# A two-layer trunk on one core: the order of loads in the S5 blocks, and the place of the y sums and low parts behind the retention masks

## The chip, the core and the metric

The kernel runs on one core of one Trainium2 chip. The metric is the device time of one launch in microseconds (us). TensorE is PE in the rows, VectorE is DVE, ScalarE is ACT, GpSimd is POOL and SyncE, whose queue issues nearly all DMAs, is SP.

## What is computed

The input is one sequence of 1024 frames with 1024 features, in fp32. Two layers are added to it, `x = x + mixer(rmsnorm(x))`, and a last rmsnorm follows. The change touches the mixer of the first layer only. Cut to what matters, it is:

```python
proj = h @ w_in                       # u, g_s5, q, k, v, g_ret
y_s5 = s5_mixer(u_s5, ...)            # diagonal complex state space, 64 groups of 16 channels
                                      # y = gelu(C x + D u); y = y * sigmoid(y @ glu_w + glu_b)
y_s5 = y_s5 * silu(g_s5)
y_ret = retention(q, k, v) * silu(g_ret)
#   scores = (q k^T) * mask;  out = scores v + (decayed q) S;  S = decay * S + kv
#   out = (out - mean) * rsqrt(var + eps), per head
return concat([y_s5, y_ret]) @ w_out
```

The second layer is a Conformer convolution module with its own projections. It stands behind all that the change touches.

## The kernel before

All of it is one class, `Trunk`. Each fp32 product is made as three products of high and low parts (`mm3`, L200 to L202: high by high, low by high, high by low), in matmuls of 128x512. An array so has a high tile (`...h`) and a low tile (`...l`), the low one being the array minus the high one.

The order of the work on each engine is not written out: a scheduler of the tile framework places the instructions by priorities and by the time of a simulated run. The code steers it with `tc.issue_after(x)`: what is issued inside that context stands behind `x`. The loads go through one queue, SP's, in the order that the scheduler gives, and each load also waits until its buffer is free (`bufs` in the tile calls).

**S5 blocks.** The state space part works in eight blocks of eight groups, while TensorE also makes the gate products `mm_g` of the input projection. For block B, `s5_states` (from L842) does this:

- it loads u (`U`, L850) from DRAM;
- TensorE makes the inputs of the states, `v`, from U and the tables W2 (L868), VectorE turns them (`m`, L876 to L881), scans them (L883) and turns them back into S (L890 to L895);
- TensorE makes a block of the convolution kernel, `kp` (L902, L903), VectorE adds the direct path to it (`Kg`, L906), TensorE transposes it (`kt`, L908), ScalarE copies it (`Kt`, L910), SP stores it to DRAM (`k_d`, L912), and a load with overlapping rows brings it back as the shifted kernel `Wd` (L915), which ScalarE copies to W1 (L917).

`s5_out` makes the block's y from W1, U, W3 and S one block later and stores it. The tables W2 of blocks 2 to 7 come from `s5_w2` (L791): four loads of 256 KB spread two small tables over the partitions (`PTr`, `PTi` at L799, `BTr`, `BTi` at L802), and six VectorE products (L806 to L811) make `W2r` and `W2i`. Each of these tiles has one buffer. The loads stand behind `self.u_load`, the load of U of the block before.

**Retention pairs.** The eight heads are worked in four pairs. `retention` (L997) makes k, q and v of a pair and then calls `ret_heads`: the scores `sp` (L1192) in two halves of the sequence, their masks on VectorE (`sc`, L1198), the output `ro` from states (L1221) and from scores (L1226), and statistics, normalization and transposes (`st`, `mv`, `on`, `rt`). `self.masked[0]` and `self.masked[1]` are the last mask of the first and of the second half. `kraw`, `krot`, `qraw` and `qrot` are the parts of the rotary embedding, `kt` at L1158 is the decayed k, and S (L1183, L1185) the state.

**The y pass.** Between the pairs the S5 output is read again, in four passes of two row blocks (`y_pass`, L947), each in three parts that are separated by `yield`: load and gelu, with the result stored to `yn_d` (L960); four sums for a Strassen-like product (L966 to L969), made in place, so that the first of them must wait until the store of `yn` has read its tile; and the split of the sums into a high part `th` (L973) and a low part (L974), both stored to `t_d` (L975, L976). In pair 2 the sums are made from `scored()` (L1029), which `ret_heads` calls when the masks of the first half have been written.

**The GLU.** `layer0_back_and_layer1` (L1264) multiplies y by the GLU weights. It loads the first quarter `y11` and the second quarter `y21` of y from `yn_d` (`load_split`, L1274: f at L1284, high part on ScalarE and low part on VectorE at L1260 and L1262), and sums of y from `t_d` (`load_sum`, L1296: `yt2`, `yt3`, 16 loads in all). The low parts of `y21` stand behind `self.last_kt`, the last `kt` of the last pair. The products with y21 are the first `mm_glu` behind the last `ro`.

## Time and profile before

| | us |
|---|---|
| runs | 1145.49, 1145.79, 1152.16; median 1145.79 |
| span of the profiled execution | 1149.0, 3.2 above the median |
| PE busy | 1125.3 (98% of the span) |
| DVE busy | 847.4 (74%) |
| POOL busy | 654.3 (57%) |
| ACT busy | 489.5 (43%) |
| longest wait of PE by line | 6.8 in two waits, at `ro` for the masks |
| mean rate of the DMA engines | 228 GB/s |

In a row of the timeline stand the start, the duration, the engine, the line and operation, what is written and read, how many instructions the row holds, and in brackets how long the engine had been idle and what ended that. A row of the waits has the engine and line that waited, what it waited for, and then the total, the number of times and the longest wait. A row of the windows has the stretch and its length, busy time with the number of instructions for PE, its weight loads, DVE, ACT and POOL, then the clock that TensorE was granted (1.00 is full speed), the mean busy share of the 16 DMA engines, and the GB/s that they moved.

### The profile page before, as it was taken

What the parts mean: (1) busy time and instruction counts of PE and PEld (TensorE: products, weight loads), DVE (VectorE), ACT (ScalarE), POOL (GpSimd) and SP (SyncE); (2) the same over time, 40 slices, a digit from 0 to 9 for tenths busy, and PEclk for the clock granted to TensorE, in tenths of its full rate; (3) what the DMA queues carried; (4) which work ended last, traced back from release to release, by engine and by line L of the source; (5) the groups of instructions that cost most, each with busy time, mean ns of one, the idle gap of its engine ahead of it and who ended that gap; (6) DMA issues with size and microseconds to landing.
All of it is one profiled execution on the core that took longest, in us unless ns stands there. A gap on an engine that the chain in (4) does not pass through costs nothing.

```text
span 1149.0 us, 17198 instructions
## 1 busy us (share of the span) xinstructions
PE 1125.3 (98%) x6286; PEld 986.1 (86%) x6286; DVE 847.4 (74%) x1464; ACT 489.5 (43%) x719; POOL 654.3 (57%) x448
## 2 busy tenths in 40 slices
PE   9999999999999999989899999999999999999997
PEld 7888878888888889889788888888888888888787
DVE  6975788887418469484669622599999889999844
ACT  6423222333223231322446523555545677444674
POOL 2059999999246354232476011489544568677663
PEclk9999999999999999989899999999999999999999
DMA  9344445556388766858999988665778755357865
GB/s 352 111 134 154 122 164 177 179 174 206 114 279 290 241 220 186 292 171 304 348 382 308 342 287 282 185 240 202 239 256 293 242 188 175 119 182 257 287 226 193
DMA packets 117636, 261.45 MB, mean 228 GB/s; under 512 B 10672, under 2 KB 42288, under 8 KB 116912
## 3 DMA queue, kind: packets, MB, share of 16 engines
q1 hardware_dynamic: 114096, 247.78, 64.1%
q10 hardware_dynamic: 3456, 12.58, 2.9%
q8 instruction: 49, 0.80, 0.3%
q14 instruction: 35, 0.29, 0.1%
HBM read 181.48 MB, written 74.65 MB: 223 GB/s over the span
## 4 chain that ended last, share of the span: by engine, by line
PE 74%; DVE 13%; DMA 5%; issue 3%; POOL 3%; ACT 2%; SPq 0%; POOLq 0%; DVEq 0%; ACTq 0%
DVE cv L1535 5%; PE mm_wo L201 5%; PE mm_wo L200 5%; PE mm_wo L202 5%; PE mm_g L200 4%; PE mm_g L201 4%; PE mm_g L202 4%; PE mm_b L201 2%; PE mm_b L202 2%; PE mm_b L200 2%; PE mm_a L202 2%; PE mm_a L201 2%; PE mm_a L200 2%; PE mm_u L202 2%; PE mm_u L200 2%
## 5 line engine op out<-in xcount | busy, mean ns | idle before, releaser
L1535 DVE SCALAR_TENSOR_TENSOR cv<-u,convw,cv 128x512 f32<-128x512 f32 x398 | 273.0, 748 | 6.8 <-ACT cv L1514 4.8
L1508 POOL TENSOR_TENSOR tp<-tp,tp 128x512 f32<-128x512 f32 x64 | 82.9, 1296 | 33.9 <-ACT tp L1507 32.8
L200 PE MATMUL mm_g<-xh,wh_g 128*128 128x512 f32 x256 | 99.4, 388 | 0.0
L201 PE MATMUL mm_g<-xl,wh_g 128*128 128x512 f32 x256 | 98.1, 383 | 0.0
L202 PE MATMUL mm_g<-xh,wl_g 128*128 128x512 f32 x256 | 97.9, 382 | 0.0
L437 POOL TENSOR_TENSOR s1q<-s1q,s1q 128x512 f32<-128x512 f32 x12 | 17.1, 1427 | 81.4 <-ACT s1q L432 81.4
L1507 ACT ACTIVATE tp<-u,convw 128x512 f32<-128x512 f32 x64 | 45.4, 719 | 35.6 <-POOL tp L1508 34.8
L200 PEld LDWEIGHTS mm_g<-xh,wh_g 128*128 128x128 f32 x256 | 48.8, 191 | 8.7 <-issue 1.2
L202 PEld LDWEIGHTS mm_g<-xh,wl_g 128*128 128x128 f32 x256 | 48.8, 191 | 7.1
L201 PEld LDWEIGHTS mm_g<-xl,wh_g 128*128 128x128 f32 x256 | 48.7, 190 | 6.9 <-issue 0.4
L190 POOL TENSOR_TENSOR wl_v<-wf_v,wh_v 128x1024 fp32r<-128x1024 f32 x12 | 31.0, 2590 | 38.0 <-ACT wh_v L189 38.0
L190 POOL TENSOR_TENSOR wl_glu<-wf_glu,wh_glu 128x1024 fp32r<-128x1024 f32 x14 | 35.1, 2506 | 30.7 <-ACT wh_glu L189 30.7
L202 PE MATMUL mm_oc<-zh,wl_woc 128*128 128x512 f32 (+1 forms) x144 | 51.0, 357 | 0.3 <-DMA wl_woc<-lo_woc 0.3
L201 PE MATMUL mm_oc<-zl,wh_woc 128*128 128x512 f32 (+1 forms) x144 | 51.1, 356 | 0.0
L200 PE MATMUL mm_oc<-zh,wh_woc 128*128 128x512 f32 (+1 forms) x144 | 50.7, 363 | 0.0
L201 PE MATMUL mm_u<-xl,wh_u 128*128 128x512 f32 x128 | 48.5, 381 | 0.7 <-DVE xl L316 0.7
L200 PE MATMUL mm_wo<-ysh,wh_wos 128*128 128x512 f32 x128 | 48.9, 382 | 0.0
L200 PE MATMUL mm_g<-h1h,wh_cg 128*128 128x512 f32 x128 | 48.9, 382 | 0.0
L201 PE MATMUL mm_b<-h1l,wh_cb 128*128 128x512 f32 x128 | 48.7, 381 | 0.1
L202 PE MATMUL mm_b<-h1h,wl_cb 128*128 128x512 f32 x128 | 48.6, 380 | 0.0
L201 PE MATMUL mm_wo<-ysl,wh_wos 128*128 128x512 f32 x128 | 48.5, 379 | 0.0
L202 PE MATMUL mm_wo<-ysh,wl_wos 128*128 128x512 f32 x128 | 48.5, 379 | 0.0
(526 smaller groups left out, 3613.3 us busy)
## 6 DMA issues: line engine op xcount, KB each, us to landing
wf_g<-w_ab SPq DMA_DIRECT2D x16, 512.0 KB
wf_wos<-w_out SPq DMA_DIRECT2D x16, 512.0 KB
wf_wor<-w_out SPq DMA_DIRECT2D x16, 512.0 KB
wf_cb<-w_c SPq DMA_DIRECT2D x16, 512.0 KB
wf_ca<-w_c SPq DMA_DIRECT2D x16, 512.0 KB
wf_woc<-w_out_c SPq DMA_DIRECT2D x16, 512.0 KB
wf_v<-w_v SPq DMA_DIRECT2D x12, 512.0 KB
wf_cg<-w_c SPq DMA_DIRECT2D x11, 512.0 KB
```

The source lines that it names most:

```text
L190: self.low_made = lo[i].tensor_tensor(wl[:].rearrange(fl)[:, c], wf[:, c], h.bitcast(F32), op=ALU.subtract)
L200: nc.tensor.matmul(ps, wh[:, kb, :], xh, start=start, stop=False, **more)
L201: nc.tensor.matmul(ps, wh[:, kb, :], xl, start=False, stop=False, **more)
L202: self.last_mm = nc.tensor.matmul(ps, wl[:, kb, :], xh, start=False, stop=stop, **more)
L437: nc.gpsimd.tensor_tensor(a, a, sq[:], op=ALU.add)
L1507: nc.scalar.mul(sk[:], u[:, k:k + HALF], cw[:, nb, k:k + 1])
L1508: gp.tensor_tensor(s0[:], s0[:], sk[:], op=ALU.add)
L1535: v.scalar_tensor_tensor(dst[:], *tap, accs_[i][:], op0=ALU.mult, op1=ALU.add)
```

## The change

Four edits, all of them to what stands behind what:

1. The load of the shifted kernel is kept as `self.wd_load`. The load of U stands behind the shifted kernel of the block before it, and the four loads of the W2 tables stand behind the last load of U and the last load of a shifted kernel.
2. In pair 2 the sums of y stand behind the masks of the second half, and are issued when these have been written.
3. The low parts of y21 stand behind the masks of the last pair's second half.
4. The loads of the sums `yt2` and `yt3` stand behind the last load of y21.

No instruction is added or removed apart from how DMA rows are grouped.

```diff
@@ plan
-        self.low_load, self.early_low = {}, None
+        self.low_load, self.early_low, self.wd_load = {}, None, None
@@ s5_w2
-        with self.tc.issue_after(self.u_load.ins):
+        with self.tc.issue_after(self.u_load.ins), self.tc.issue_after(self.wd_load.ins):
@@ s5_states
-        self.u_load = nc.sync.dma_start(U[:], self.u_d[B].rearrange("j h g m -> (j h) g m"))
+        with self.tc.issue_after(self.wd_load.ins) if self.wd_load else nullcontext():
+            self.u_load = nc.sync.dma_start(U[:], self.u_d[B].rearrange("j h g m -> (j h) g m"))
...
-        nc.sync.dma_start(Wd[:], bass.AP(tensor=kd.tensor, offset=kd.offset, ap=[[P, P], [16 * P, 8], [1, P]]))
+        self.wd_load = nc.sync.dma_start(
+            Wd[:], bass.AP(tensor=kd.tensor, offset=kd.offset, ap=[[P, P], [16 * P, 8], [1, P]]))
@@ retention, scored()
-                    with self.tc.issue_after(self.masked[0].ins):
+                    with self.tc.issue_after(self.masked[1].ins):
@@ ret_heads
-            if hf == 0:
+            if hf == 1:
                 scored()
@@ load_split
-                nc.sync.dma_start(f, part)
+                self.part_load = nc.sync.dma_start(f, part)
@@ load_sum
-        def load_sum(name, i, c, h):
+        def load_sum(name, i, c, h, behind=None):
...
-                    nc.sync.dma_start(o[:].bitcast(F32), self.t_d[i, j, rows(k), hs(c)])
+                    with self.tc.issue_after(behind.ins) if behind else nullcontext():
+                        nc.sync.dma_start(o[:].bitcast(F32), self.t_d[i, j, rows(k), hs(c)])
...
-        b11, b21 = load_split(B(0, 0), "y11", 0, True, None, self.last_v), load_split(B(1, 0), "y21", 0, True, self.last_kt, self.last_v)
+        b11, b21 = load_split(B(0, 0), "y11", 0, True, None, self.last_v), load_split(B(1, 0), "y21", 0, True, self.masked[1], self.last_v)
+        y21_load = self.part_load
...
-                    t2, t3 = (load_sum("yt2", 0, 0, 1), None) if m == 0 else (t2, load_sum("yt3", 1, 1, 1))
+                    t2, t3 = (load_sum("yt2", 0, 0, 1, y21_load), None) if m == 0 else (t2, load_sum("yt3", 1, 1, 1, y21_load))
```

Three places show how the rows move. (Line numbers behind the change are 1 to 4 higher.) The first is SP's queue in the S5 blocks, from the store of block 2's kernel on; `Wd_1678` is block 2's shifted kernel, `U_1886` is block 3's u, `PTr_1870` and its like are the tables for block 3 and `PTr_2135` and its like those for block 4. Before:

```order
L912 DMA k_d<-Kt_1675 128x128
L915 DMA Wd_1678<-k_d 128x8x128
L850 DMA U_1886<-u_d 128x1024
L799 DMA PTr_2135<-pt_d 128x1x512
L802 DMA BTr_2137<-bt_d 128x1x512
L799 DMA PTi_2136<-pt_d 128x1x512
L802 DMA BTi_2138<-bt_d 128x1x512
```

After:

```order
L913 DMA k_d<-Kt_1675 128x128
L916 DMA Wd_1678<-k_d 128x8x128
L799 DMA PTr_1870<-pt_d 128x1x512
L802 DMA BTr_1872<-bt_d 128x1x512
L799 DMA PTi_1871<-pt_d 128x1x512
L802 DMA BTi_1873<-bt_d 128x1x512
L851 DMA U_1886<-u_d 128x1024
```

The tables loaded behind a block's kernel are now those of the next block; before they were those of the block after it. U, for the next block too, went behind them.

The second is VectorE in pair 2, from the last mask of the first half to the last of the second (`sc_2_4660` and `sc_2_4661`, read from `sp_2_4678` and `sp_2_4679` before and from `sp_2_4674` and `sp_2_4675` after, are the second masks). Before:

```order
L1198 TENSOR_TENSOR sc_2_4661<-sp_2_4663,retmask_4009 128x512
L966 TENSOR_TENSOR yn_4620<-yn_4620,yn_4615 128x512
L1065 TENSOR_TENSOR kraw_4848<-mm_k_0_4849,R_354 128x512
L967 TENSOR_TENSOR yn_4615<-yn_4615 128x512
L968 TENSOR_TENSOR yn_4615<-yn_4620,yn_4615 128x512
L1198 TENSOR_TENSOR sc_2_4660<-sp_2_4678,retmask_4009 128x512
L1198 TENSOR_TENSOR sc_2_4661<-sp_2_4679,retmask_4009 128x512
```

After:

```order
L1200 TENSOR_TENSOR sc_2_4661<-sp_2_4663,retmask_4009 128x512
L1067 TENSOR_TENSOR kraw_4848<-mm_k_0_4849,R_354 128x512
L1200 TENSOR_TENSOR sc_2_4660<-sp_2_4674,retmask_4009 128x512
L1200 TENSOR_TENSOR sc_2_4661<-sp_2_4675,retmask_4009 128x512
L968 TENSOR_TENSOR yn_4620<-yn_4620,yn_4615 128x512
L969 TENSOR_TENSOR yn_4615<-yn_4615 128x512
```

The sums of y (L966 to L968 before, L968 to L970 after) went from ahead of the second masks to behind them.

The third is SP at the end of the last y pass. Before, from the last pair of the `yt2` loads on (three pairs more stand ahead of it, behind the last store of the sums):

```order
L1302 DMA yt2h_5518<-t_d 128x512
L1302 DMA yt2l_5519<-t_d 128x512
L1302 DMA yt3h_5604<-t_d 128x512
L1302 DMA yt3l_5605<-t_d 128x512
L1284 DMA y21f_5468<-yn_d 128x512 x2
```

After, from the last store of the sums on:

```order
L978 DMA t_d<-yn_5210 128x1024
L1286 DMA y21f_5468<-yn_d 128x512 x2
L1330 DMA yg_0_5566<-gs_d 128x512
L1332 DMA yn_0_5568<-yn_d 128x512
L1332 DMA yn_0_5592<-yn_d 128x512
L1286 DMA y21f_5479<-yn_d 128x512 x2
L1305 DMA yt2h_5506<-t_d 128x512
L187 DMA wf_glu_5500<-w_glu 128x1024
```

The y21 loads (two rows of two loads each) went ahead of all loads of the sums.

## The prediction

> **What bounds the kernel now.** I read the page's head first, then the waits of PE, then the timelines of PE and of the engine that each wait names.
>
> ```profile
> span 1149.0 us, 17198 instructions
> PE 1125.3 (98%) x6286; PEld 986.1 (86%) x6286; DVE 847.4 (74%) x1464; ACT 489.5 (43%) x719; POOL 654.3 (57%) x448
> ```
>
> PE is busy for 98% of the span, so only what makes it wait, or makes its matmuls slow, can give time back. The waits say where:
>
> ```profile
> PE ro L1221 <- DVE sc L1198: 6.8, 2, 4.5
> PE kt L908 <- DVE Kg L906: 2.0, 1, 2.0
> PE ro L1221 <- DVE S L1185: 1.9, 1, 1.9
> ```
>
> Three places: the kernel transpose `kt` in one S5 block, and the state products `ro` in two retention pairs. The edits touch what VectorE does ahead of each.
>
> *Gap 1, S5 block 2.* PE's timeline, the first state matmuls `v` of blocks 1 to 4:
>
> ```profile
> 126.56 0.66 PE L868 MATMUL v<-U,W2r 128*64 128x128 f32 x8
> ...
> 149.30 1.09 PE L868 MATMUL v<-U,W2r 128*64 128x128 f32 x16
> ...
> 180.72 0.98 PE L868 MATMUL v<-U,W2r 128*64 128x128 f32 x14
> ...
> 208.21 0.99 PE L868 MATMUL v<-U,W2r 128*64 128x128 f32 x14
> ```
>
> A block takes 208.21 − 180.72 = 27.49 us undisturbed, and 180.72 − 149.30 = 31.42 here: 3.93 lost, though PE waited only 2.0. The windows after the wait, from 162.2 on, hold the rest:
>
> ```profile
> 162.20:163.90 1.70, 1.70 (x5) 1.34 (x5) 1.70 (x3) 0.00 (x0) 1.70 (x3) 0.50 0.00 0
> 163.90:165.60 1.70, 1.70 (x5) 1.33 (x4) 1.70 (x2) 0.00 (x0) 1.62 (x2) 0.50 0.00 0
> ```
>
> The granted clock (third column from the end) was 0.50 for 3.4 us, which costs half of that, 1.7. VectorE was late because of what stood in front of it:
>
> ```profile
> 155.67 1.59 DVE L806 TENSOR_TENSOR W2r<-PTr,BTr 128x512 f32<-128x512 f32 x1
> 157.19 0.68 DVE L876 TENSOR_TENSOR m<-v,Ts 128x512 f32<-128x512 f32 x1
> ...
> 160.99 0.16 DVE L906 TENSOR_TENSOR Kg<-kp,s_s_dd 128x16 f32<-128x16 f32 x1
> ```
>
> Table products for the next block (L806, and L807 between `m` and `Kg`) run ahead of `Kg`, for which PE waits.
>
> *Gap 2, retention pair 2.* PE, pair 1 (undisturbed) and pair 2, from the second half's `ro` to the next projection:
>
> ```profile
> 442.91 1.16 PE L1221 MATMUL ro<-S,qrot 64*128 64x128 f32 x16
> ...
> 445.81 0.46 PE L200 MATMUL mm_q<-xh,wh_q 128*128 128x512 f32 x1
> ```
>
> ```profile
> 486.85 0.48 PE L1221 MATMUL ro<-S,qrot 64*128 64x128 f32 x2
> 491.82 2.07 PE L1221 MATMUL ro<-S,qrot 64*128 64x128 f32 x14 [4.49 <-DVE sc L1198]
> 497.00 0.46 PE L200 MATMUL mm_k<-xh,wh_k 128*128 128x512 f32 x1
> ```
>
> Undisturbed it is 445.81 − 442.91 = 2.90; here 497.00 − 486.85 = 10.15; 7.25 lost. PE's wait is 4.49 of it; much of the rest is again a slow clock, since 14 matmuls of L1221 take 2.07 where 16 took 1.16. VectorE:
>
> ```profile
> 487.61 0.69 DVE L966 TENSOR_TENSOR yn<-yn,yn 128x512 f32<-128x512 f32 x1 [4.76 <-DMA yn_d<-yn]
> ...
> 491.09 1.27 DVE L1198 TENSOR_TENSOR sc<-sp,retmask 128x512 f32<-128x512 f32 x2
> ```
>
> The second masks stood behind the sums of y, and the first sum stood 4.76 us waiting for a store.
>
> *Gap 3, pair 3.*
>
> ```profile
> 550.03 0.48 PE L1221 MATMUL ro<-S,qrot 64*128 64x128 f32 x2 [1.91 <-DVE S L1185]
> ...
> 558.21 0.46 PE L200 MATMUL mm_glu<-y21h,wh_glu 128*128 128x512 f32 x1
> ```
>
> PE was free at 550.03 − 1.91 = 548.1, and the GLU could have begun 2.90 later, at 551.0. It began at 558.21: 7.2 lost. What VectorE stood at, and why:
>
> ```profile
> 547.78 0.69 DVE L1262 TENSOR_TENSOR y21l<-y21f,y21h 128x512 fp32r<-128x512 f32 x1 [5.01 <-ACT y21h L1260]
> ```
> ```profile
> 547.13 1.29 ACT L1260 CAST y21h<-y21f 128x512 fp32r<-128x512 f32 x2 [9.88 <-DMA y21f<-yn_d]
> ```
> ```profile
> 534.21 1.53 SPq L1302 DMA_DIRECT2D yt2h<-t_d  x1
> ...
> 541.80 0.91 SPq L1284 DMA_DIRECT2D y21f<-yn_d  x2
> ```
>
> The quarter of y was loaded behind ten loads of sums, 7.6 us after SP began on them. All three: 3.9 + 7.25 + 7.2 = 18.4 us, the most that the change can bring here.
>
> **Part 1, shifted kernel ahead of u (gap 1).** On SP the store of `k_d` and the load of `Wd` come first, then the four PT/BT loads, then U; but these four loads now serve the next block, where before they were one block ahead. On VectorE the six table products so stand behind `Kg` and the scan, and gap 1's cause is gone: 3.93 back. The new risk is that W2 is ready too late for `v`. For block 2, from SP's rows of before:
>
> ```profile
> 138.89 0.33 SPq L912 DMA_DIRECT2D k_d<-Kt  x1
> ...
> 140.51 0.41 SPq L915 DMA_DIRECT2D Wd<-k_d  x1
> ```
>
> `k_d` waits for VectorE's scan, from which three products (about 3 us, rows below) go away, and for `kt`, which stands 3 matmuls earlier; I take 137.2 (estimate; between 135.9, all 3 us, and 138.9, none). Wd follows 1.6 later, 138.8; BTi is issued last of the four, about 141.2. What must land is 1.5 MB and the 0.5 MB gate store beside it; the core moved
>
> ```profile
> 140.00:150.00 10.00, 10.00 (x55) 8.57 (x57) 8.52 (x12) 0.63 (x1) 9.84 (x7) 1.00 0.82 239
> ```
>
> 239 GB/s there: 2 MB in 8.4 us from 138.8 is 147.2, and at the 391 GB/s of the fullest stretch (below) 144. I take 146. Then the products follow:
>
> ```profile
> L807 DVE TENSOR_TENSOR W2i<-PTr,BTi x6: 678/1514/1619, 131.0 to 268.3; 128x512 f32<-128x512 f32 x6
> ...
> L808 DVE TENSOR_TENSOR PTr<-PTi,BTi x6: 773/1456/1853, 134.4 to 270.2; 128x512 f32<-128x512 f32 x6
> L809 DVE TENSOR_TENSOR PTi<-PTi,BTr x6: 667/876/1006, 137.3 to 273.7; 128x512 f32<-128x512 f32 x6
> ...
> L810 DVE TENSOR_TENSOR W2r<-W2r,PTr x6: 1581/1866/1886, 137.9 to 274.5; 128x512 f32<-128x512 f32 x6
> ...
> L811 DVE TENSOR_TENSOR W2i<-W2i,PTi x6: 1342/1574/1760, 144.4 to 279.3; 128x512 f32<-128x512 f32 x6
> ```
>
> By the medians 1.51 + 0.6 (a gate product stands between) + 1.46 + 0.88 + 1.87: W2r at 152.3, W2i at 153.9. PE wants W2r behind 9 more matmuls than before (four in 1.7 us at half clock, above, so 0.21 each at full), at 149.3 + 1.9 = 151.2, and W2i some 0.9 later, behind half of `v`. Late by 1.1 and 1.7: a new wait of 1.7 (0 if the loads land by 144; 3.5 if only at 147.8). The late start leaves block 3 less room: 0.4 more (0 to 1). In later blocks the same chain ends 152.3 − 126.6 = 25.7 and 27.3 us after the block's own `v`, wanted at 27.5 and 28.4: covered by 1.1. Gap 1 then brings 3.93 − 2.1 = **1.8** (−0.6 to 3.9).
>
> Here a rule can be weighed. The clock rows above follow an idle stretch of 2.0 us. The Trainium skill (TensorE: Matmul & The Clock Gate, "HAM oscillation — how this bites in real kernels") says: 'The abstract rule is "no PE-idle gaps >~3.4µs."' By it gap 1 would have cost no clock, and its term would be 2.0 − 2.1 = −0.1 instead of 1.8. The trace disagrees: 2.0 us sufficed for 0.50.
>
> **Part 2, sums of y behind the second masks (gap 2).** The masks no longer meet the wait for the store; they take 1.27 and need only the scores, which PE writes ahead of the first half's `ro`. In pair 1, where nothing stands before them, they are in time, and here only one `kraw` does. All 7.25 is won at that place. What is late next: pair 3's VectorE.
>
> ```profile
> 520.62 0.74 DVE L966 TENSOR_TENSOR yn<-yn,yn 128x512 f32<-128x512 f32 x1 [4.04 <-DMA yn_d<-yn]
> ...
> 531.81 0.69 DVE L973 CAST th<-yn 128x1024 fp32r<-128x1024 f32 x1 [6.41 <-DMA t_d<-th]
> 532.54 1.23 DVE L974 TENSOR_TENSOR yn<-yn,th 128x1024 fp32r<-128x1024 f32 x1
> 535.15 1.29 DVE L1158 TENSOR_TENSOR kt<-ktp,kdec 128x512 f32<-128x512 f32 x2 [1.38 <-PE ktp L1156]
> ```
>
> The products L1158, which PE's `kv` needs, stand behind the last y pass, a chain of loads, gelus and stores that does not move with PE; before it was done 1.38 us early. Now PE comes 7.25 earlier. The chain changes by itself: its store of y stands behind one more transfer (1 later: 521.6), but the y and row loads that shared the 6.41 us wait are now issued before it. From 521.6, the four sums and the first cast (3.5) and a store of some 3.5 (VectorE waited 4.04 for the one before L966), then 0.69 + 1.23: 530.5 against 533.77. L1158 so moves from 535.15 to 530.6, 4.55, and PE waits 7.25 − 4.55 = 2.7 (0 if the chain is 3 us quicker, 5.9 if it doesn't move). 2.7 is more than the 2.0 that dropped the clock, but may be cut by a window's end: half of 1.7, 0.85. Term: 7.25 − 2.7 − 0.85 = **3.7** (−0.3 to 7.25).
>
> **Parts 3 and 4, low parts of y21 and loads of the sums (gap 3).** On SP the four y21f loads come first, so they issue when the last stores of the y pass are out, some 3 us earlier than the 534.21 of the row above, with a few small loads between, 531.5 to 535, instead of 541.8 and later; loading to cast took 5.3 before (541.80 to 547.13), so casts at about 537 to 541. On VectorE the low parts stand behind both masks; four of 0.69 are done by about 544. PE wants them at 551.0 − 1.8 − 3.7 = 545.5: covered by 1.5. The yt2/yt3 loads, now behind, are read only by the GLU's later products; the DMA engines are what they meet:
>
> ```profile
> 550.00:560.00 10.00, 7.65 (x40) 7.05 (x41) 9.21 (x41) 4.87 (x8) 2.91 (x2) 0.66 1.04 391
> ```
>
> They are full there (share 1.04). PE comes 12 us earlier and the first of these loads about as much; I price a late weight at 0.7 (0 to 3.6, half of the gap). Term: 7.2 − 0.7 = **6.5** (3.6 to 7.2). After the GLU PE's waits are few and on other work, so what is won stays.
>
> **Sum.** 1.8 + 3.7 + 6.5 = 12.0. The profiled execution would take 1149.0 − 12.0 = 1137.0. The three runs have a median of 1145.79, 3.2 below the profiled span; the losses are waits that recur, so the forecast for the median is 1145.79 − 12.0 = 1133.8.
>
> **Rivals.**
> - *Nothing new waits.* The loads land by 144 and the y pass moves with PE: all 18.4 are won, 1127.4. For it: every new wait above hangs on an estimate of DMA time. Against: SP issues PT/BT a block later.
> - *The y pass and the DMA engines take it back.* The chain ends at 533.77 as before: gap 2 gives 7.25 − 5.9 − 1.7 = −0.3; half of gap 3 goes to late GLU loads, 3.6 left; with 1.8, 5.1 in all: 1140.7. For it: a DMA share above 1.0; against: fewer loads stand before the store.
> - *Slower: W2 late in every block.* If PT/BT land x later than I take, block 2 waits 1.7 + x and blocks 3 to 7 each x − 1.1, and from some 2 us of wait each adds 1.7 of slow clock. With x = 4.2 (2 MB at 160 GB/s) this is 5.9 + 1.7 + 5 × (3.1 + 1.7) = 31.6 against 3.9 + 3.7 + 6.5 = 14.1 gained: 17.5 slower, 1163. It decides from about x = 2.6, where the waits reach 4.3 + 1.7 + 5 × 1.5 = 13.5 (above some 2 us a slow clock comes on top). Against: landing at 148.6 would be 10 us after Wd's issue.
> - *The change doesn't do what it says.* Where the masks leave the wait for the store, the statistics behind it inherit it and the transposes of `ro` and the next gate follow late: PE's next stop takes what gap 2 gave, and gap 1 is swapped for block 2's wait. At most 3 of gain: 1143.
>
> **How the numbers follow.** Forecast (1129 to 1138) 0.55; nothing new 0.12; taken back 0.22; no effect 0.05; slower 0.06. A measurement of this kernel tells about 1% (11.5 us, 1134.3) from no change. Faster by over 1%: all of the 0.12, and 0.38 of the forecast's 0.55: 0.50. Slower by over 1%: 0.05, nearly all of that rival. Within: 0.45. The range 1126.5 to 1141.5 takes in the first two rivals' values and leaves out no effect, slower, and some tails.
>
> **What would show each step.** Right: `kt` no longer among PE's waits, and a wait of 1 to 2 us at `v` in block 2 alone; `ro` without a wait on `sc` in pairs 2 and 3; a wait of some 3 us before pair 3's `kv`, on L1158; the GLU's first y21 matmul at about 545. Wrong: waits at `v` in blocks 3 to 7 (part 1); `kv` at 536 as before (part 2); waits of `mm_glu` on ACT or DMA beyond 1 us in all (parts 3 and 4).

## The result, and the profile after

The changed kernel takes 1180.14 us (median of 4 runs, 1177.3 to 1182.23), the kernel before 1147.45 (4 runs beside it): 1.028 times as long, 95% interval 1.0242 to 1.0317, or 32.7 us more. The profiled execution of after has a span of 1176.9 and took 1178.76 as a run, 1.4 below its median. By the same 1.8 around the span, the profiled execution of before (1149.0) lies 3 us above its own median, so the two spans show 27.9 of the 32.7.

The head of the page after:

```profile
span 1176.9 us, 17179 instructions
PE 1131.5 (96%) x6286; PEld 989.3 (84%) x6286; DVE 838.9 (71%) x1464; ACT 488.7 (42%) x719; POOL 646.6 (55%) x448
```

PE's waits after, longest first:

```profile
PE v L869 <- DVE W2r L810: 23.0, 5, 6.8
PE mm_v L1114 <- ACT v L1117: 3.9, 1, 3.9
PE cst L509 <- DVE cs L1621: 3.6, 1, 3.6
PE mm_glu L200 <- ACT mm_glus L1341: 1.8, 1, 1.8
PE mm_glu L200 <- ACT sg L1341: 1.7, 1, 1.7
```

The three waits that the change was aimed at, `kt` for `Kg` and `ro` for `sc` and for S, are gone from the list. A wait more than twice as large as all three stands in their place: the first state matmuls `v` wait for the last table product. PE's timeline shows the stop at `v` in every block from 2 to 7 (in block 4 the profile names no releaser, "issue"):

```profile
157.81 1.98 PE L869 MATMUL v<-U,W2r 128*64 128x128 f32 x16 [6.79 <-DVE W2r L810]
188.91 1.09 PE L869 MATMUL v<-U,W2r 128*64 128x128 f32 x16 [3.22 <-DVE W2r L810]
219.24 1.09 PE L869 MATMUL v<-U,W2r 128*64 128x128 f32 x16 [1.21 <-issue]
253.11 1.98 PE L869 MATMUL v<-U,W2r 128*64 128x128 f32 x16 [6.13 <-DVE W2r L810]
284.28 1.09 PE L869 MATMUL v<-U,W2r 128*64 128x128 f32 x16 [1.21 <-DVE W2r L810]
317.70 1.98 PE L869 MATMUL v<-U,W2r 128*64 128x128 f32 x16 [5.68 <-DVE W2r L810]
```

The blocks now start 31.1, 30.3, 33.9, 31.2 and 33.4 us apart, where an undisturbed block took 27.49. Behind the long waits the 16 matmuls take 1.98 instead of 1.09, at a granted clock of 0.50, as the windows behind block 2's wait show (third column from the end):

```profile
158.00:160.00 2.00, 2.00 (x21) 2.00 (x21) 2.00 (x3) 0.63 (x1) 0.00 (x0) 0.50 0.00 0
160.00:162.00 2.00, 2.00 (x26) 1.67 (x27) 0.44 (x2) 0.00 (x0) 0.00 (x0) 0.50 0.75 264
```

How far PE is behind the kernel before, read off the same instruction in the two profiled executions, gives the balance of the whole change:

| instruction of PE | before | after | behind by | since the row above |
|---|---|---|---|---|
| `v` of block 7 | 290.67 | 317.70 | 27.0 | part 1 |
| `rt` ahead of gap 2 | 459.72 | 490.04 | 30.3 | 3.3 lost, with the rest of S5 |
| `mm_k` behind gap 2 | 497.00 | 520.07 | 23.1 | 7.25 won |
| `ktp` of pair 3 | 534.51 | 563.39 | 28.9 | 5.8 given back |
| `mm_glu` with y21, behind gap 3 | 558.21 | 579.82 | 21.6 | 7.3 won |
| first `mm_wo`, behind the GLU | 625.39 | 651.58 | 26.2 | 4.6 given back |
| `mm_oc` near the end | 1080.07 | 1108.14 | 28.1 | 1.9 lost |

### The profile page after: what moved, and what is told of

It is laid out like the page before. It is cut to its first block, busy times and chain, and to the rows that moved or that the text cites. A ratio compares the mean times of both kernels' runs of the same rounds, so it can differ in the third digit from the quotient of the medians.

```text
span 1176.9 us, 17179 instructions
## 1 busy us (share of the span) xinstructions
PE 1131.5 (96%) x6286; PEld 989.3 (84%) x6286; DVE 838.9 (71%) x1464; ACT 488.7 (42%) x719; POOL 646.6 (55%) x448
## 4 chain that ended last, share of the span: by engine, by line
PE 41%; DVE 6%; POOL 2%; DMA 2%; issue 2%; ACT 1%; POOLq 0%; DVEq 0%
PE mm_wo L201 5%; PE mm_wo L202 5%; PE mm_wo L200 5%; DVE cv L1539 4%; PE mm_b L201 2%; PE mm_b L200 2%; PE mm_b L202 2%; PE mm_a L202 2%; PE mm_a L200 2%; PE mm_a L201 2%; PE mm_glu L202 2%; PE mm_glu L200 2%; PE mm_glu L201 2%; PE mm_oc L202 1%; PE mm_oc L201 1%
## 5 line engine op out<-in xcount | busy, mean ns | idle before, releaser
L1512 POOL TENSOR_TENSOR tp<-tp,tp 128x512 f32<-128x512 f32 x64 | 83.0, 1297 | 33.7 <-ACT tp L1511 32.7
L394 ACT ACTIVATE gt<-gt 128x512 f32<-128x512 f32 x32 | 20.1, 628 | 96.3 <-DVE gt L393 96.3
L190 POOL TENSOR_TENSOR wl_v<-wf_v,wh_v 128x1024 fp32r<-128x1024 f32 x12 | 32.4, 2702 | 31.2 <-ACT wh_v L189 31.2
L202 PE MATMUL mm_a<-h1h,wl_ca 128*128 128x512 f32 x128 | 48.6, 380 | 0.0
```

The lines of the kernel that those rows point to most:

```text
L190: self.low_made = lo[i].tensor_tensor(wl[:].rearrange(fl)[:, c], wf[:, c], h.bitcast(F32), op=ALU.subtract)
L202: self.last_mm = nc.tensor.matmul(ps, wl[:, kb, :], xh, start=False, stop=stop, **more)
L394: nc.scalar.activation(gt[:, c], gt[:, c], AF.Silu)
L1512: gp.tensor_tensor(s0[:], s0[:], sk[:], op=ALU.add)
```

## Experiments

All ratios are against the kernel before on the same chip. The times are medians; the ratio, with its 95% interval, is estimated from all runs and can differ from that of the medians in the third decimal. "Ahead" and "behind" compare one profiled execution with the one of the kernel before, which lay some 3 us above its median, so a lead of 3 us in them is no gain yet.

### The parts one by one

Part 1 alone (`s5_w2`, `s5_states`), part 2 alone (`scored`), parts 3 and 4 alone, and part 3 alone. Then the whole change without one line:

```diff
-        with self.tc.issue_after(self.u_load.ins), self.tc.issue_after(self.wd_load.ins):
+        with self.tc.issue_after(self.u_load.ins):
```

> Only the first part: U behind the shifted kernel, the tables' loads (PT, BT) behind both. Theory A (the tables of the next block are now loaded inside the block, behind the shifted kernel, and land some 10 to 14 us after its issue, so the state products v wait for W2 in blocks 2 to 7): the whole loss of the S5 stage stays, +27 to +30 us, and the rest of the kernel is as before: about 1174 to 1177 against 1147. Rival B (the loss is a sum over all three places, the S5 blocks with some 15): +12 to +18.

Part 1 alone: 1178.09 against 1147.73, ratio 1.0256 [1.0227, 1.0285].

```profile
PE v L869 <- DVE W2r L810: 20.8, 6, 6.6
```

> Only the second part: sums of y in pair 2 behind the second masks. In the changed kernel the distance to before shrank by 7 us at this place and grew by 5.8 at pair 3's values, where ScalarE's copies stood behind a gelu that waited for its load. Theory: so it goes here too, 7 won and 5 to 6 given back at mm_v: -1 to -2 us. Rival: the gelu was late only because the S5 stage had pushed its stores and loads, and without that part nothing is given back: -7 us.

Part 2 alone: 1148.02, 1.0002 [0.9979, 1.0025]. It won 6.6 at `mm_k` (490.40 against 497.00) and was 3.3 behind at `ktp`, so 9.9 were given back. PE's largest wait names the place:

```profile
PE mm_v L1112 <- ACT v L1115: 7.7, 1, 7.7
```

> Only the third and fourth parts: low parts of y21 behind the last masks, loads of the sums behind y21's. Theory: gap 3 goes (-7.2) and the GLU gives back some 4 to 5 us, since ScalarE's sigmoids and the weights come late for a PE that is early: -2 to -3.5 us. Rival (the GLU's loss in the changed kernel came of the other parts): -7 us.

Parts 3 and 4: 1149.5, 1.001 [0.9985, 1.0034]. At the first y21 product PE was 13.5 ahead (7.3 of it won there), at `mm_wo` 5.7: the GLU gave 7.8 back.

> The third part alone: low parts of y21 behind the last masks, but the loads of the sums ahead of y21's loads as before. Theory D (the GLU gave back gap 3 because the later loads of the sums and of the gates pushed each other on full DMA engines): here the loads keep their order, so the masks come in time, the GLU starts once y21's low parts are made, some 5 us earlier than before, and less is given back: 1143 to 1145. Theory S (given back because the statistics of ro and ScalarE's table change, which ran beside the stall, now stand ahead of the first sigmoid): as with both parts, no gain, 1147 to 1150.

Part 3 alone: 1150.45 against 1147.99, 1.0027 [1.0008, 1.0045]; 8.9 ahead at the first y21 product, 2.0 at the y11 products that follow (561.45 against 563.47), and 1.3 behind at `mm_wo`.

> The changed kernel without one edge: the tables' loads stand behind the load of U alone, as before, so that they are again issued a block ahead; U stays behind the shifted kernel, and the other parts stay. Theory A: the waits at v for W2 vanish, and the time falls by 25 to 30 us, to 1143 to 1150. Rival C (U, issued behind the shifted kernel, is what v waits for, and the named W2 only came last by little): v goes on waiting, now for U, and more than 10 us of the loss stay: above 1157.

All but the table edge: 1149.43, 1.0016 [0.9993, 1.0039], with no wait at `v`. The three parts sum up: 30.4 + 0.3 + 1.8 = 32.5 of the 32.7 measured; each has an interval of about ±3, so that the sum fits this closely is partly luck. The one line on the PT/BT loads makes nearly all of it.

### Why the tables land late

Each of these five is part 1 alone, with one thing changed. First, the loads of U of blocks 2 to 7, which share the DMA engines with the tables, are left out:

```diff
-        U = w.tile([P, 8, P], F32, name=f"U_{B}", tag="U", bufs=2)
-        with self.tc.issue_after(self.wd_load.ins) if self.wd_load else nullcontext():
-            self.u_load = nc.sync.dma_start(U[:], self.u_d[B].rearrange("j h g m -> (j h) g m"))
+        U = self.U1 if B > 1 else w.tile([P, 8, P], F32, name=f"U_{B}", tag="U", bufs=2)
+        self.U1 = U
+        if B < 2:
+            with self.tc.issue_after(self.wd_load.ins) if self.wd_load else nullcontext():
+                self.u_load = nc.sync.dma_start(U[:], self.u_d[B].rearrange("j h g m -> (j h) g m"))
```

> The first part alone, and the loads of U of blocks 2 to 7 left out (these blocks compute on block 1's u, so y is not the reference's): 0.5 MB less per block, issued right behind the tables. In the run with the first part alone the tables of block 3 were issued within 2 us behind the shifted kernel and the last landed 14 us behind it, while 3 MB moved at some 225 GB/s. Theory A1 (the tables share the 16 DMA engines with all that is queued beside them, also what is issued behind them): the last table lands some 2 us earlier, and the waits at v fall by about 2 us in each of six blocks, 10 to 14 us in all: 1163 to 1168. Theory A2 (the tables are slow by themselves, by their own rows or place in the queue): no change, 1175 to 1180.

1178.56 (2 runs) against 1147.99, 1.0272 [1.0225, 1.032]: no change. BTi was issued at 141.42 and its first reader could start only 10.6 us later:

```profile
152.03 0.69 DVE L807 TENSOR_TENSOR W2i<-PTr,BTi 128x512 f32<-128x512 f32 x1 [2.12 <-DMA BTi<-bt_d]
```

So sharing the engines with U is not the cause. (A weight load came in U's place, at 142.09; the next run has both behind the tables.) The loads themselves differ from a weight load in two ways: they read 8 or 16 rows over and over (a step of 0), and the slowest dimension of their source has only 8 steps. The next run took both away, with plain rows of a weight array of the same size, U and the weight behind them as in part 1 (W2 is then no longer made from the tables):

```diff
-                                          ap=[[32 * P, 8], [0, 16], [1, 4 * P]]))
...
-                                          ap=[[0, 8], [32 * P, 16], [1, 4 * P]]))
+                nc.sync.dma_start(pt[:].rearrange("p q n -> p (q n)"), self.A["w_ab"][4 * c].rearrange("p k n -> p (k n)")[:, :4 * P])
+                nc.sync.dma_start(bt[:].rearrange("p q n -> p (q n)"), self.A["w_ab"][4 * c + 1].rearrange("p k n -> p (k n)")[:, :4 * P])
```

> The first part alone, with each of the four table loads reading a plain block of a weight array of the same size (128 rows of 2 KB, all different), where the tables' own loads read 8 or 16 rows of 2 KB again and again for all partitions (W2, and so y, is not the reference's). In the run without U's loads the last table still landed 10.6 us after its issue, and the DMA engines were busy for less than 0.7 at the end of it. Theory R (the repeated reads of the same few rows are what is slow): the last table lands in some 5 to 6 us, the waits at v fall by 4 to 5 us a block and nearly vanish: 1150 to 1156. Theory B (what is ahead of them is slow: the shifted kernel of 1024 rows of 512 bytes on the same queue, and the stores of the gate and of y beside): no change, 1175 to 1180.

1160.99 (2 runs) against 1150.15, 1.01 [1.0073, 1.0126]. BTi, issued at 141.30, was there after 5.8 us:

```profile
147.11 1.16 DVE L803 TENSOR_TENSOR W2i<-PTr,BTi 128x512 f32<-128x512 f32 x1 [0.53 <-DMA BTi<-w_ab]
```

Block 7's `v` was 8.7 us behind the kernel before, where part 1 alone was 23.3 behind. Two more runs separated the two differences. Repeated rows with 16 steps:

```diff
-                                          ap=[[32 * P, 8], [0, 16], [1, 4 * P]]))
+                                          ap=[[32 * P, 16], [0, 8], [1, 4 * P]]))
...
-                                          ap=[[0, 8], [32 * P, 16], [1, 4 * P]]))
+                                          ap=[[32 * P, 16], [0, 8], [1, 4 * P]]))
```

> Part 1 with the four table loads each reading 16 rows of bt_d, each row repeated for 8 partitions in a row, so that the rows are still read many times over but the slowest dimension of the source has 16 steps, not 8 (the values are not the reference's tables; W2 and what follows from it is not either). Two theories of the slow landing. Repeated rows (reading one row of DRAM for many partitions is slow in itself): the last table lands 10 to 11 us after its issue, as in part 1 with U left out (141.42 to 152.03), the loss in S5 stays near 27 to 30 us, ratio 1.024 to 1.029. Eight engines (a load whose slowest source dimension has 8 steps runs on 8 of the 16 DMA engines; the Trainium skill, DMA: Bandwidth & Descriptors, Rules for kernel authors, states that a slowest dimension below 16 confines a DMA to so many engines at most): lands within 5.5 to 7 us, as with plain rows (141.30 to 147.11), and the ratio is 1.008 to 1.012.

1169.42 against 1150.16, 1.0177 [1.0137, 1.0217], between the two theories: BTi issued at 141.46, its product at 150.22, 8.8 later; block 7's `v` 15.4 behind. And distinct rows in 8 groups, with a row left out between the groups:

```diff
+                    wa = self.A["w_ab"][4 * c + n]
+                    nc.sync.dma_start(x[:].rearrange("p q n -> p (q n)"),
+                                      bass.AP(tensor=wa.tensor, offset=wa.offset,
+                                              ap=[[17 * KB * P, 8], [KB * P, 16], [1, 4 * P]]))
```

> Part 1 with the four table loads reading 128 distinct rows of w_ab, in 8 groups of 16 rows with one row left out between the groups, so that no row is read twice but the slowest dimension of the source has 8 steps (the tables' values are not the reference's, nor is W2). Repeated rows: as with the plain rows, the last table lands some 5.8 us after its issue, ratio 1.008 to 1.012. Eight engines: lands 9 to 11 us after its issue, DMA rate about 200 to 240 GB/s while the tables load, ratio 1.022 to 1.029.

1174.66, 1.0225 [1.0175, 1.0275]: as slow as part 1 within the intervals, with no row read twice. BTi issued at 141.83, its product at 153.12, 11.3 later; block 7's `v` 23.1 behind, against 23.3 for part 1. The windows of the two kernels with distinct rows, the one with plain rows (128 steps) first, then that with 8 (the last column is GB/s):

```profile
144.00:146.00 2.00, 2.00 (x12) 1.73 (x10) 0.56 (x1) 1.88 (x3) 2.00 (x2) 1.00 1.03 392
146.00:148.00 2.00, 2.00 (x11) 1.76 (x10) 1.47 (x2) 0.25 (x1) 1.92 (x3) 1.00 1.01 407
```

```profile
144.00:146.00 2.00, 2.00 (x11) 1.73 (x11) 0.00 (x0) 1.57 (x3) 2.00 (x2) 1.00 0.85 229
146.00:148.00 2.00, 2.00 (x11) 1.76 (x10) 0.00 (x0) 0.56 (x2) 1.92 (x3) 1.00 1.04 199
```

About half the rate: the 8 steps are enough to make the landing late. The busy share of the DMA engines (the column ahead of the GB/s) doesn't tell the two apart. The traces also hold the signals by which a load reports its end, and these do: BTi's end came in 16 signals with plain rows (146.49 to 147.09) and with 16 steps, but in 8 with 8 steps, here (152.90 to 153.10) as in the changed kernel (152.41 to 152.66), behind a single one right after the issue. The end of a load with 8 steps was so reported in half as many parts.

Repeating rows costs less, but not nothing: with 16 steps the core still moved only this much in one stretch, and 6.7 us more were lost by block 7 than with plain rows.

```profile
146.00:148.00 2.00, 2.00 (x11) 1.76 (x10) 0.00 (x0) 0.22 (x1) 2.00 (x2) 1.00 0.85 104
```

Part of that may be that the four loads of this run share rows (`PTr` and `BTr` read the same 16, `PTi` and `BTi` another 16); this wasn't taken apart.

### Why plain tables were still 11 us late

With plain rows, what is left could be the chain from `Wd` over the loads and six products to `v`, or U behind the tables. Plain rows, and two of the six products left out (W2r then also no longer needs `PTi` and `BTi`, the last two loads, so that its chain gets shorter by more than two products):

```diff
-        v.tensor_tensor(ptr[:], pti[:], bti[:], op=ALU.mult)
-        v.tensor_tensor(pti[:], pti[:], btr[:], op=ALU.mult)
```

> Part 1 with the table loads reading plain rows of w_ab, and two of the six table products left out as well (those that write PTr and PTi), so W2 and what hangs on it are not the reference's. With plain reads and all six products the first v of blocks 2 to 7 lagged 3.8, 2.2, 4.3, 5.9, 7.7, 8.7 us behind the kernel before, and the kernel stood at 1.010. Chain theory (what is left of the loss is that shifted kernel, table loads and six products together still take longer than a block's 27.5 us): two products of 1.6 and 1.5 us less make the chain 3.1 us shorter, below 27.5; no wait at v of more than 0.5 us, block period 27.5, lag at block 7's v between -4 and 0 (gap 1 is won), ratio 0.996 to 1.001. Rival (what is left is the load of U behind the tables, or VectorE's other work): the waits at v stay at 1 to 2 us in each block, lag at block 7 of 6 to 9, ratio about 1.008 to 1.010.

1146.71 against 1146.96, 0.9997 [0.9977, 1.0018]. Blocks 3 to 7 start 27.49 us apart again, with no wait at `v`; the only one left is of 1.2, for W2i in block 2:

```profile
205.11 1.09 PE L863 MATMUL v<-U,W2r 128*64 128x128 f32 x16
...
232.60 1.09 PE L863 MATMUL v<-U,W2r 128*64 128x128 f32 x16
...
260.08 1.09 PE L863 MATMUL v<-U,W2r 128*64 128x128 f32 x16
```

PE is 3.1 us ahead of the kernel before from block 3's `v` to the end of S5, and was 0.6 ahead at block 2's: 2.5 of gap 1's 3.9 are won in the trace, as soon as the chain fits into a block, though the median shows no gain. The chain theory holds: U stands behind the tables here too, and nothing waits for it.

The other way to win gap 1 keeps the early loads and puts only the first two products behind the `Kg` of the block before:

```diff
-        v.tensor_tensor(w2r[:], ptr[:], btr[:], op=ALU.mult)
-        v.tensor_tensor(w2i[:], ptr[:], bti[:], op=ALU.mult)
+        with self.tc.issue_after(self.last_kg.ins):
+            v.tensor_tensor(w2r[:], ptr[:], btr[:], op=ALU.mult)
+            v.tensor_tensor(w2i[:], ptr[:], bti[:], op=ALU.mult)
...
-        v.tensor_tensor(Kg[:, :16], kp[:, :16], self.dd[:, B, :], op=ALU.add)
+        self.last_kg = v.tensor_tensor(Kg[:, :16], kp[:, :16], self.dd[:, B, :], op=ALU.add)
```

> The kernel before, with only the two first table products of a block (L806, L807) put behind the Kg of the block before it; all loads as before. Theory: gap 1 goes (its idle 2.0 us always, its slow clock in those executions in which the clock's window falls so), and nothing becomes late, since the tables had landed long before: 2 to 4 us faster, 1143 to 1146. Rival (the two products then delay the scan, the copy of the kernel and its store, and v or y waits): no gain or a loss of 1 to 3.

3.6 us ahead after gap 1 and 2.8 at the end in the profiled execution, but 1148.3 against 1147.99, 1.0008 [0.9989, 1.0027]: the medians show no gain.

### Where gaps 2 and 3 went

Part 2 gave its gain back where ScalarE's copies of `mm_v` stood behind the last gelu of the y pass. To see whether that gelu is the bound or only the first in line, part 2 with the gelu behind the third copy of v:

```diff
-            with self.tc.issue_after((self.last_v if i else self.third_v).ins) if k == 2 else nullcontext():
+            with self.tc.issue_after((self.last_v if i and k == 2 else self.third_v).ins) if k == 2 or (k == 3 and i) else nullcontext():
```

> The second part alone, and the last gelu of the last y pass put behind the third of ScalarE's value copies of pair 3, instead of ahead of the first. Theory (PE's values waited 7.7 us because those copies stood behind a gelu that waited for its load): the wait of mm_v on v vanishes. The y pass ends where it did, so pair 3's kt product is late by some 3 us instead: of the 9.9 us that were given back, 6 to 7 stay won, 1140 to 1143. Rival (the load of y bounds that stretch whatever the order): the wait only moves, to kv or to the GLU's first product, and the time stays at 1147 to 1149.

1147.81 against 1147.99, 1.001 [0.9995, 1.0024]. The wait at `mm_v` is gone and stands at `kv`:

```profile
PE kv L1175 <- DVE kt L1158: 9.2, 1, 9.2
```

That is the place of the prediction: the chain of the y pass sets the pace, and `mm_v` was only its first meeting with PE. Next, also the sums and splits of pair 3 behind its `kt`, and then parts 3 and 4 added:

```diff
-                if pair != 2:
+                if pair < 2:
                     next(parts)
-                if pair in (0, 3):
+                if pair == 0:
                     next(parts, None)
...
                 if pair == 3:
+                    with self.tc.issue_after(self.last_kt.ins):
+                        next(parts)
+                        next(parts, None)
                     early.close()
```

> The second part and the gelu behind the third value copy, and in pair 3 the sums of y and their split put behind the kt product instead of ahead of it. Theory (the y pass's chain of load, gelu, store and sums gave back gap 2 because PE needs kt, which stood behind it: 9.2 us of wait at kv when only the gelu was moved): the wait at kv goes to below 2 us, and the chain ends in the shadow of pair 3's scores: 6 to 7 us won before the GLU, some of it lost in the GLU: 1141 to 1145. Rival (the sums, now between the states and the masks of pair 3, hold those up by their wait for the store): ro waits 3 us or more, and nothing is won.

> The same as the run with the sums behind kt, with the third and fourth parts as well (all of the change but its S5 part, and with the y pass out of kt's way). Theory D (in the GLU the DMA engines are full from the first y21 load on, so PE can't end it earlier by more than the loads let it): the GLU begins 10 to 14 us earlier than before and ends 2 to 5 us earlier: 1142 to 1146. Theory S (what is given back in the GLU is only the sigmoid's wait for the statistics, 2 to 3 us): 1136 to 1140.

1150.87 against 1150.15, 1.0016 [0.9998, 1.0034], and 1153.96, 1.004 [1.0017, 1.0063]. Now retention ends early (5.9 and 11.0 us in the table below), and the GLU takes it all back. Would the GLU keep it if the DMA engines were free? 24 of the 32 loads of sums were left out (all products with sums read `yt2`), in parts 3 and 4, in the kernel before as a control, and in the last kernel above (the GLU then computes with other sums):

```diff
-                    t2, t3 = (load_sum("yt2", 0, 0, 1, y21_load), None) if m == 0 else (t2, load_sum("yt3", 1, 1, 1, y21_load))
+                    t2, t3 = (load_sum("yt2", 0, 0, 1, y21_load), None) if m == 0 else (t2, t2)
...
-        t4 = load_sum("yt4", 1, 0, 0)
+        t4 = t2
...
-                t1 = load_sum("yt1", 0, 1, 0)
+                t1 = t2
```

> The third and fourth parts, with 24 of the 32 loads of sums left out (yt3, yt4 and yt1 are replaced by yt2's tiles, so the GLU is not the reference's): 6.3 MB less between about 545 and 590 us. Theory D (full DMA engines are why the GLU ends where it did although it begins 7 us earlier): the GLU keeps its lead: 5 to 8 us below the control run with the same loads left out of the kernel before. Theory S (the waits for ScalarE's table change and statistics, and VectorE's queue, give it back whatever the loads do): 0 to 2 us below that control.

> Control: the kernel before with the same 24 loads of sums left out (the GLU is not the reference's). PE waits for none of them before, so theory D and theory S both expect little from it by itself, 0 to 3 us faster (gap 3 is a bit shorter, since the loads of y21 stand behind fewer others).

> All but the S5 part, the y pass out of kt's way, and the same 24 loads of sums left out (the GLU is not the reference's). With all loads this began the GLU some 20 us earlier and ended it where before did. Theory D: most of that lead stays, 10 to 18 us below the control. Theory S: within 3 us of the control.

Against 1146.82: 1154.34, 1.0052 [1.003, 1.0074]; 1156.44, 1.0088 [1.0062, 1.0113]; 1154.64, 1.0068 [1.0049, 1.0088]. Leaving loads out made the control slower: PE's products stand in the same order, but VectorE makes low parts of y22 ahead of gate products `gu` (L1384), for which PE then waits 5.1 us in two waits. Beside this control the edits gain about 2 us, which is within the intervals, and not the 5 to 18 that were expected if full DMA engines were the reason. PE's last `ro` and first `mm_wo` in the profiled executions:

| kernel | last `ro` | first `mm_wo` |
|---|---|---|
| before | 557.76 | 625.39 |
| part 2 | 557.68 | 628.79 |
| parts 3 and 4 | 542.91 | 619.72 |
| part 2 and gelu behind v | 554.31 | 623.57 |
| the same, sums behind `kt` | 551.82 | 623.34 |
| the same, and parts 3 and 4 | 546.73 | 626.89 |
| before, few sums | 548.67 | 627.95 |
| all of these, few sums | 545.76 | 624.76 |

The end of retention moves by 15 us, the end of the GLU by 9, and the two don't go together. Full DMA engines are not the reason: in the last kernel of the table the windows of the GLU (second last column: share) show them partly free, and PE waits all the same (first column behind the length). In the kernel before, PE was busy for all of 580 to 600 with the share at 1.04.

```profile
580.00:600.00 20.00, 18.66 (x86) 15.71 (x85) 17.97 (x17) 7.93 (x12) 14.09 (x7) 1.00 0.76 240
600.00:620.00 20.00, 15.97 (x71) 12.78 (x70) 16.07 (x25) 13.13 (x21) 12.80 (x8) 1.00 0.88 290
```

What PE waits for there differs from kernel to kernel. Parts 3 and 4, with all loads of sums:

```profile
PE mm_glu L200 <- DVE gu L1386: 2.7, 2, 1.6
...
PE mm_glu L200 <- ACT sg L1339: 1.7, 1, 1.7
PE mm_glu L200 <- ACT mm_glus L1339: 1.4, 1, 1.4
```

and all but S5, with all loads of sums (the two long ones of the first row's waits stand between the last `ro` and the first y21 product):

```profile
PE rt L1252 <- DVE on L1244: 7.0, 3, 3.3
...
PE mm_glu L200 <- DVE mm_gluz L1403: 2.3, 1, 2.3
PE mm_glu L200 <- DVE gu L1389: 1.3, 1, 1.3
PE mm_glu L202 <- POOL wl_glu L190: 1.1, 1, 1.1
```

These are gates, sums and low parts on VectorE, ScalarE and GpSimd, with VectorE busy for 16 to 18 of 20 us in the windows above. Which of them would have to go for the GLU to end earlier stays open; no edit here brought a gain that shows in the medians, and no version was faster than the kernel before by more than its interval.

## Why the prediction was wrong

**Part 1, the step that failed: the landing of the tables.** Everything ahead of it came as worked out; PE was ready for `v` at 151.0, where the sum had 151.2. SP's rows after, beside the forecast of 137.2, 138.8 and 141.2:

```profile
137.39 0.33 SPq L913 DMA_DIRECT2D k_d<-Kt  x1
138.93 0.38 SPq L916 DMA_DIRECT2D Wd<-k_d  x1
...
141.49 0.58 SPq L802 DMA_DIRECT2D BTi<-bt_d  x1
```

Then "I take 146" met this on VectorE:

```profile
148.97 1.15 DVE L806 TENSOR_TENSOR W2r<-PTr,BTr 128x512 f32<-128x512 f32 x1 [8.39 <-DMA BTr<-bt_d]
152.68 1.25 DVE L807 TENSOR_TENSOR W2i<-PTr,BTi 128x512 f32<-128x512 f32 x1 [2.56 <-DMA BTi<-bt_d]
```

The last table was there at 152.7, 11.2 us after its issue and 6.7 later than taken. The estimate divided bytes by a rate of the whole core: 2 MB by 239 GB/s. The rate of after was about that,

```profile
146.00:148.00 2.00, 2.00 (x11) 1.76 (x10) 0.00 (x0) 0.26 (x1) 1.92 (x3) 1.00 1.07 206
148.00:150.00 2.00, 2.00 (x11) 1.73 (x11) 1.03 (x1) 0.00 (x0) 1.92 (x3) 1.00 1.02 224
```

but more than 2 MB went through at that rate before the tables were there: the trace's DMA summary from 139 to 154 has

```profile
DMA packets 2059, 3.35 MB, mean 224 GB/s; under 512 B 88, under 2 KB 1112, under 8 KB 2059
```

with U and a weight, issued behind the tables, among it. That these took the tables' share is excluded: plain rows landed in 5.8 us with the same two loads behind them, and without U the tables landed nearly as late (10.6 us). The way up to 391 GB/s, which the choice of 146 leaned on, was closed to these loads: their slowest source dimension has 8 steps. Distinct rows with 8 steps landed 11.3 us after issue at 199 to 229 GB/s, with 128 rows 5.8 us after issue at 392 to 407. The Trainium skill (DMA: Bandwidth & Descriptors, "Rules for kernel authors") states that a slowest dimension below 16 confines a DMA to at most that many of the 16 engines, and names a leading step of 0 as an example; the two runs agree in size, with about half the rate and half as many signals of the end, though no view here shows single engines. The access patterns stood in the code of before, and this rule spoke against the change; there the loads were a block ahead and their landing could not be seen in any wait.

**"Covered by 1.1" in later blocks** fell with it. The margin per block was so thin that 6.7 us more broke it in all six blocks, which is the rival "W2 late in every block", deciding from x = 2.6, given 0.06. Even plain rows didn't fit. The sum took the chain from block 1's `v` to W2r, 25.7 us, as "the same chain" for the later blocks, wanted at 27.5. With plain rows it took 26.6 behind block 1's `v`, but 28.4 to 29.8 behind those of blocks 2 to 6. The products are not what was short: from the second one to the end of W2r it is 4.5 to 5.9 us in five blocks and 7.3 in one, where the sum had 6.3. The chain began later, with `Kg` 4.5 us behind block 1's `v` and 6.0 to 8.6 behind those of blocks 2 to 6, since VectorE still had the last product, gate products and the low part of a weight ahead of it. Block 1 (its `v` began at 126.37) and block 3 (182.95):

```profile
130.86 0.17 DVE L903 TENSOR_TENSOR Kg<-kp,s_s_dd 128x16 f32<-128x16 f32 x1
```

```profile
182.77 1.59 DVE L807 TENSOR_TENSOR W2i<-W2i,PTi 128x512 f32<-128x512 f32 x1
184.28 1.28 DVE L393 TENSOR_TENSOR gt<-mm_g,R 128x512 f32<-128x512 f32 x2
186.60 1.91 DVE L190 TENSOR_TENSOR wl_g<-wf_g,wh_g 128x1024 fp32r<-128x1024 f32 x1 [1.04 <-ACT wh_g L189]
...
190.82 0.16 DVE L903 TENSOR_TENSOR Kg<-kp,s_s_dd 128x16 f32<-128x16 f32 x1
```

So a second term was short, by 2.7 to 4.1 us a block against the 25.7, and this alone used up the 1.1 of room.

With x = 6.7 the rival's own formula gives 10.1 + 5 × 7.3 = 46.6 of loss, and 33.5 were lost (29.6 behind at the first `mm_k` after S5, 351.49 against 321.93, with gap 1's 3.9 won). (Its own example has a slip: 2 MB at 160 GB/s from 138.8 land at 151.3, so x is 5.3, not 4.2, and the kernel would be 24 slower, not 17.5.) The formula added the slow clock to each wait. But once `v` waits for the chain in each block, the chain sets the distance of the blocks (30.3 to 33.9 us), and matmuls at half clock only shorten the next wait. This is read from the rows, and was not tried by itself.

**Part 2: 3.7 forecast, about nothing measured** (1.0002). The 7.25 were won at the spot in the changed kernel, and 6.6 in part 2 alone; that the first agrees to the hundredth is luck. "The products L1158, which PE's `kv` needs, stand behind the last y pass, a chain of loads, gelus and stores that does not move with PE" was the right mechanism. It failed in place and size: ScalarE met the chain first. The gelu of the y pass stood idle, and the copies of `mm_v` stood behind it (the row names no releaser; in part 2 alone the gelu began at 520.08, and its load had landed at 520.01):

```profile
545.92 1.92 ACT L960 ACTIVATE yn<-yp 128x1024 f32<-128x1024 f32 x1 [5.49 <-issue]
547.75 1.19 ACT L1117 ACTIVATE v<-mm_v,Rtok 128x256 f32<-128x256 f32 x3
```

5.8 were given back instead of 3.55 (2.7 of wait and 0.85 of clock), about what the range's upper end has for the wait (5.9, the chain not moving at all); in part 2 alone it was 9.9. The term that was mis-sized is the start of the sums. The sum let them begin 1 us later than before, at 521.6, and end the chain at 530.5. In part 2 alone:

```profile
525.26 1.45 DVE L966 TENSOR_TENSOR yn<-yn,yn 128x512 f32<-128x512 f32 x1 [12.83 <-issue]
...
533.01 1.23 DVE L974 TENSOR_TENSOR yn<-yn,th 128x1024 fp32r<-128x1024 f32 x1
```

They began 4.6 later. From there the chain took 9.0, as worked out (8.9), and it ended at 534.2, where before it ended at 533.8. Part 2 alone, and the gelu moved away, show that removing one meeting point only brings up the next.

**Parts 3 and 4: 6.5 forecast.** Won at the first y21 product: 7.3, as worked out. The 0.7 for the GLU was the term that was mis-sized: 4.6 in the changed kernel, 7.8 with parts 3 and 4 alone, above the 3.6 of the range. The rival took full DMA engines as the reason; the runs with few sums speak against that, and what took it instead stays open.

**The sum** went wrong by the S5 term: +1.8 forecast, −30.4 measured. The other two, 10.2 forecast together, measured −0.3 and −1.8, each with an interval of about ±2.9 (0.0025 of 1148). Taken for granted was also that "the losses are waits that recur": single executions of the kernel before ranged from 1141.65 to 1155.35 over two chips, so a gain of 3 us in one trace need not be one in the median, as the run with the products behind `Kg` shows.

## What to carry to other kernels

Before a load is put on a chain that sets the end, look at its access pattern, not only at its bytes: loads with 8 steps in their slowest dimension took twice the time of loads with 128 here, unseen as long as they were a block ahead. Add up the whole chain of a repeated block, everything that stands between on the same engine with it, against the block's length; where the margin is a twentieth of a block, a miss is paid in every block, and the gain only once. A wait that is removed gains nothing until the next engine that paces the stage is earlier too.

## What the runs showed of the hardware that was not expected

- The last of four loads of 256 KB with a source of 8 steps landed 11.2 us after its issue (11.3 with no row read twice, 8.8 with 16 steps and repeated rows), in the same traffic where plain rows took 5.8. Its end came in 8 signals instead of 16.
- The clock's drop did not follow the length of a wait alone. In the changed kernel, after waits of 6.79, 6.13 and 5.68 us the next 16 matmuls ran at half clock (1.98 us); after one of 3.22 they began at full clock (1.09 us), and the clock fell only then, as the first window shows, while ahead of the change a wait of 2.0 us was followed by 3.4 us at 0.50. In part 1 alone, waits of 3.02 and 2.92 at `v` in blocks 3 and 4 were followed by no drop at all (the last two rows). The rival's "from some 2 us of wait each adds 1.7 of slow clock" does not hold for these.

```profile
190.00:192.00 2.00, 2.00 (x29) 1.67 (x28) 0.97 (x3) 1.95 (x3) 0.00 (x0) 0.51 0.00 0
```

```profile
189.00:195.00 6.00, 5.93 (x64) 5.19 (x65) 4.96 (x6) 2.35 (x4) 3.16 (x2) 1.00 0.25 91
219.50:225.50 6.00, 5.95 (x64) 5.21 (x65) 4.96 (x7) 2.35 (x4) 3.19 (x3) 1.00 0.13 51
```
